# Third pair's right-half weight sums on VectorE, GpSimd's accumulates in program order, and every output transfer on SyncE's queue

## The chip, the cores and the metric

The kernel runs on one NeuronCore of one Trainium2 chip. The metric is the device time of one launch in microseconds (us), as a median over timed runs; lower is better. A core has five engines with queues of their own: PE (TensorE, matrix products), DVE (VectorE), ACT (ScalarE), POOL (GpSimd) and SP (SyncE, here only a queue that issues transfers). Each works through its own instructions in order and waits on semaphores that others raise. Sixteen DMA engines carry the transfers that SP, ACT and POOL issue.

## What is computed

A decoder layer for one sequence of 512 tokens and width 1024. Only its end matters here, the feed-forward part:

```
h = rmsnorm(x, g_pre_ffn) * (1.0 + sc2) + sh2
u = relu(h @ w_ff1)                    # 512 x 4096
y = (u * u) @ w_ff2                    # 512 x 1024, in float32
x = x + ga2 * rmsnorm(y, g_post_ffn)   # the output
```

## The kernel before, in words

All matrix products keep float32 accuracy by splitting each operand into a rounded high part and a rest: `split` (L111 to L113) lets ACT write the high part (L112) and DVE the rest (L113), and PE multiplies high by high, high by rest and rest by high.

The last product, with `w_ff2`, is done by a seven-product (Strassen-like) scheme over 2 x 2 blocks. The 4096 inner rows are 16 **pairs** p = 0 to 15 (`NP`). Its first stage makes four products of each pair (24 matmuls of 128x512), its second stage the other three (18 matmuls). Before the matmuls of a pair, `first_ops(p)` (L869) prepares the operands:

- `ah`: the token side, split from the tile `ub` (whose blocks A11, S1, S3, S2 were written by earlier steps);
- `h1, l1`: split of the left half of the weights `x = xw[p]`, and of the sum `t2` (L882, written over blocks A11 and S1 of `ub`);
- `h2, l2`: split of `n = nw[p]`, the sum of the pair's weights and of its right-half weights (`w_right[p]`). It feeds the second and third product of the pair (p5 and p7); the first (p1) needs only `ah` and the left half of `h1, l1`.

The sum `n` is made in two ways. For pairs 0 and 1 both terms are loaded by SP into `st` tiles (`stage`, L106, three buffers in rotation) and DVE adds them (L878). For pairs 2 to 15, `column_sums(p)` (L864) lets ACT copy the loaded weights into a `wn` tile (L866, three buffers) and POOL issue a transfer that adds `w_right[p]` into it in flight (L867): an accumulating transfer of 512 KB. `load(j)` loads the weights of step j, 512 KB, through SP.

`fourth_sum(p)` (L898) is another accumulating transfer of POOL, of 256 KB, into blocks A11 and S1 of the pair's `ub`, once the first stage of that pair has read them; `second_ops(p)` (L901) needs it in the second stage.

In this part of the kernel the order of DVE, ACT and PE is the order of the code (`manual_schedule`, L840). POOL is not in that list: the framework places its instructions where they can go by its own reckoning, so that a `fourth_sum` stands behind the weight sums of about the same time, though the code calls it much later. SP's transfers stand in the order of the code.

At the end, `end` (L1007) scales and adds one of the four token tiles in two halves on DVE (L1011) and sends each half off at once (L1012): the first half through SP's queue, the second through ACT's. ACT's other work there is the sum of squares of the next halves (`square`, L960), one line of which DVE's next step waits for.

Of the kernel before, what the change touches and what calls it, by code (L numbers as in the profile page):

```python
# [37 lines left out]
WBUF = 4  # L38
LAST = 3
NP = MF // 2  # L40
HB = L // 2
A11, S1, S3, S2, A12, A22 = range(6)
EARLY = 4
# [21 lines left out]
def layer_kernel(tc, x, ada, vecs, c_row, rope, w_first, w_v, w_b, w_a, w_gate, w_up, w_out, w_ff1, w_ff2, w_right, out):  # L65
    nc = tc.nc
    es = ExitStack()
    with es:
# [5 lines left out]
        def uid(name):  # L74
            cnt[0] += 1
            return f"{name}_{cnt[0]}"
# [29 lines left out]
        def stage(src, w=D):  # L106
            st = per.tile([P, D], F32, name=uid("st"), tag="st", bufs=3)
            nc.sync.dma_start(st[:, :w], src)
            return st
# [112 lines left out]
        m_es = ExitStack()  # L222
# [408 lines left out]
        m_es = ExitStack()  # L631
# [22 lines left out]
        for m in range(KT):  # L654
# [5 lines left out]
            for ps, oh, ol, c0 in ((pb, obh, obl, 512), (pa, oah, oal, 0)):  # L660
                for k in range(4):
                    cs = slice(c0 + k * P, c0 + (k + 1) * P)
# [35 lines left out]
        x1 = [x1p.tile([P, D], F32, name=f"x1_{t}") for t in range(NT)]  # L698
# [91 lines left out]
        def block_tile(name, dt):  # L790
            return u2p.tile([P, 6 * HB], dt, name=uid(name), tag="ub", bufs=NP)

        blocks = [block_tile("ub", F32) for p in range(NP)]
        f2p = es.enter_context(tc.tile_pool(name="f2p", bufs=1, side="right"))
# [3 lines left out]
        def blk(p, a, n=1):  # L798
            return blocks[p][:, a * HB:(a + n) * HB]

# [36 lines left out]

        f3p = es.enter_context(tc.tile_pool(name="f3p", bufs=1))
        m_es = ExitStack()
        m_es.enter_context(tc.manual_schedule(engines={mybir.EngineType.DVE, mybir.EngineType.Activation, mybir.EngineType.PE}))  # L840
        p1, p6, p5, p7 = [[bank(a), bank(b)] for a, b in (("tr", "tr"), ("s", "o"), ("s", "s"), ("mm", "mm"))]
        H0, H1 = slice(0, 512), slice(512, D)

# [15 lines left out]
        xw, nw, firsts, seconds = {}, {}, {}, {}  # L859

        def load(j):
            xw[j] = stage(w_ff2[2 * j]) if j < NP else stage(w_ff2[2 * (j - NP) + 1])

        def column_sums(p):  # L864
            nw[p] = ntile().bitcast(F32)
            nc.scalar.activation(nw[p], xw[p], AF.Copy)  # L866
            nc.gpsimd.dma_start(nw[p], w_right[p], accum_op=ALU.add)  # L867

        def first_ops(p):  # L869
            a = pair_tile(p, "ah")  # L870
            x, n = xw[p], nw[p]
            (h1, l1), (h2, l2) = wtile(), wtile()
            t2 = blk(p, 0, 2)
            if p != 1:
                split(a[:, 0], a[:, 1], blk(p, 0, 4))
            split(h1[:, H0], l1[:, H0], x[:, H0])
            if p < 2:
                nc.vector.tensor_tensor(n, n, x, op=ALU.add)  # L878
            if p == 1:
                split(h2, l2, n)  # L880
                split(a[:, 0], a[:, 1], blk(p, 0, 4))
            nc.vector.tensor_tensor(t2, n[:, H1], x[:, H0], op=ALU.add)  # L882
            if p != 1:
                split(h2, l2, n)
            split(h1[:, H1], l1[:, H1], t2)
            nc.vector.tensor_tensor(blk(p, S2), blk(p, A12), blk(p, S2), op=ALU.add)  # L886
            firsts[p] = (a[:, 0], a[:, 1]), (h1, l1), (h2, l2)

        def first_products(p):
            a, w1, w2 = firsts.pop(p)  # L890
            order = [(p1, A11, w1, H0), (p5, S1, w2, H0), (p7, S3, w2, H1), (p6, S2, w1, H1)]
            if p in (0, NP - 1):
                order = [order[i] for i in ((0, 1, 3, 2) if p == 0 else (0, 3, 1, 2))]
            for acc, b, w, cs in order:
                for i in range(2):
                    product(acc, i, a, b * HB, w, cs, p == 0, p == NP - 1)

# [3 lines left out]
        def second_ops(p):  # L901
            if p:
                a = block_tile("a2", F32R)
                ah, al = a[:, :3 * HB], a[:, 3 * HB:]
            else:
                a = pair_tile(0, "ah")
                ah, al = a[:, 0, :3 * HB], a[:, 1, :3 * HB]
            y, n, w = xw[NP + p], ntile(), wtile()
            t2 = blk(p, 0, 2)
# [5 lines left out]
        def second_product(acc, c0, w, cs, p, i):  # L915
            a = seconds[p][0]
            product(acc, i, a, c0 * HB, seconds[p][w], cs, False, p == NP - 1, True)

# [7 lines left out]
        nw[1] = stage(w_right[1])  # L926
        load(2)
        for p in range(NP):
            if p + 1 < NP:
                first_ops(p + 1)  # L930
                if p == 0:
                    load(3)
                    column_sums(2)
            if p == NP - 1:
                second_ops(0)
            load(p + 4)
            if 0 < p < NP - 3:
                if p == 1:
                    column_sums(3)
                column_sums(p + 3)  # L940
            for i in range(2 * (p - NP + 3), 2 * (p - NP + 4)):
                if i >= 0:
                    fourth_sum(i)
            first_products(p)
# [39 lines left out]
        ov = out.rearrange("(t p) d -> t p d", p=P)  # L984
# [22 lines left out]
        def end(t, last, bias):  # L1007
            r = rstd_of(last, bias)
            for n in range(2):
                cs = (H0, H1)[n]  # L1010
                nc.vector.scalar_tensor_tensor(x1[t][:, cs], parts[t, n], r, x1[t][:, cs], op0=ALU.mult, op1=ALU.add)  # L1011
                (nc.sync, nc.scalar)[n].dma_start(ov[t][:, cs], x1[t][:, cs])  # L1012

        def end_low(t):
            parts[t, 1] = c22[:, t % 2]
# [96 lines left out]
```

## Time and profile before

| | us |
|---|---|
| median of 3 timed runs (806.66 to 810.06) | 808.34 |
| the profiled execution | 806.59 |
| its span in the trace | 804.8 |
| PE busy | 767.5 (95%) |
| DVE busy | 593.3 (74%) |
| ACT busy | 416.7 (52%) |
| POOL busy | 29.3 (4%) |

The span is cut by PE's matmuls: the first stage of the seven-product scheme runs from 631.3 to 728.8 us, the second to 794.4, and what is left to 804.8 is DVE's and ACT's end of the norm with the output transfers. PE is the bound wherever its matmuls follow each other without a gap; a gap in them names the place where something else bounds. In a row of the trace, the first two numbers are start and duration in us, and the square bracket at its end is how long the engine had been idle and what ended it.

### The profile page before, as it was taken

The numbers are of one execution on the slowest core, as the hardware profiler recorded it, in microseconds if no ns is written. First come the engines' busy times: TensorE is split into PE (matmuls) and PEld (weight loads), VectorE is DVE, ScalarE is ACT, GpSimd is POOL, SyncE is SP. The second block draws the span as 40 slices with busy tenths as digits, with TensorE's granted clock in tenths as the row PEclk, the third lists the DMA queues.
The fourth block names the chain that finished last, engine by engine and source line by source line (L and its number), as shares of the span: only waits on it lengthen the run. The fifth ranks groups of instructions, "written<-read, shape, count | busy, mean of one in ns | idle before, by whom it ended". The sixth has DMA issues, their size and how long they took to land.

```text
span 804.8 us, 10879 instructions
## 1 busy us (share of the span) xinstructions
PE 767.5 (95%) x4014; PEld 636.4 (79%) x4014; DVE 593.3 (74%) x1111; ACT 416.7 (52%) x753; POOL 29.3 (4%) x45
## 2 busy tenths in 40 slices
PE   6999999989899999999999999999999979999994
PEld 5889977668889887887678998888888758778883
DVE  6876799999957677787866965555545567889866
ACT  6555657564637668622336843322322366768742
POOL 0000000000000000000000000000000122320000
PEclk9999999999999999999999999999999999999998
DMA  9943201122131210477782343444332489996312
GB/s 353 382 120 105 79 27 53 54 78 80 54 105 53 79 53 27 137 258 251 256 301 79 105 131 109 153 157 142 120 104 73 94 172 232 229 235 190 136 54 104
DMA packets 32596, 111.17 MB, mean 138 GB/s; under 512 B 3872, under 2 KB 3872, under 8 KB 32544
## 3 DMA queue, kind: packets, MB, share of 16 engines
q1 hardware_dynamic: 27504, 97.87, 35.4%
q0 software_dynamic: 4320, 11.54, 8.2%
q10 hardware_dynamic: 720, 1.08, 0.4%
q8 instruction: 31, 0.51, 0.3%
q14 instruction: 21, 0.17, 0.1%
HBM read 108.38 MB, written 2.10 MB: 137 GB/s over the span
## 4 chain that ended last, share of the span: by engine, by line
PE 59%; DVE 17%; DMA 10%; issue 8%; ACT 3%; POOL 2%; SPq 0%; ACTq 0%; DVEq 0%; POOLq 0%
PE mm L139 23%; PE s L139 18%; PE o L139 6%; PE mm L857 3%; DVE wlo L113 3%; DVE a L485 3%; DMA wn<-in_w_right_dram 3%; PE s L857 2%; DVE isc L411 2%; DVE sm L410 2%; DMA st<-in_ada_dram 2%; PE tr L857 2%; DMA st<-in_w_gate_dram 2%; ACT whi L112 2%; DVE be L487 2%
## 5 line engine op out<-in xcount | busy, mean ns | idle before, releaser
L112 ACT ACTIVATE whi<-st 128x1024 fp32r<-128x1024 f32 (+3 forms) x118 | 116.3, 988 | 162.1 <-DMA st<-in_w_up_dram 43.2
L113 DVE TENSOR_TENSOR wlo<-st,whi 128x1024 fp32r<-128x1024 f32 (+3 forms) x118 | 133.6, 1135 | 63.1 <-ACT whi L112 62.9
L139 PE MATMUL mm<-hTh,whi 128*128 128x512 f32 x192 | 78.2, 407 | 0.1
L139 PE MATMUL mm<-hTh,wlo 128*128 128x512 f32 x192 | 75.3, 392 | 0.0
L139 PE MATMUL mm<-hTl,whi 128*128 128x512 f32 x192 | 75.1, 391 | 0.0
L139 PE MATMUL mm<-whi,hTh 128*128 128x256 f32 (+2 forms) x208 | 62.2, 305 | 0.1
L212 DVE CUSTOM_DVE_ANT_0 st<-st,cb,vec 128x1024 f32<-128x1024 f32 x32 | 40.8, 1283 | 27.5 <-DMA st<-in_ada_dram 27.4
L139 PE MATMUL mm<-whi,hTl 128*128 128x256 f32 (+2 forms) x208 | 60.2, 295 | 0.0
L139 PE MATMUL mm<-wlo,hTh 128*128 128x256 f32 (+2 forms) x208 | 60.1, 295 | 0.0
L139 PE MATMUL s<-h2h,whi 128*128 128x512 f32 (+1 forms) x120 | 43.4, 361 | 0.0
L139 PE MATMUL s<-h2l,whi 128*128 128x512 f32 (+1 forms) x120 | 43.3, 361 | 0.0
L139 PE MATMUL s<-h2h,wlo 128*128 128x512 f32 (+1 forms) x120 | 43.3, 361 | 0.0
L139 PEld LDWEIGHTS mm<-hTh,wlo 128*128 128x128 f32 x192 | 36.0, 188 | 7.7
L139 PEld LDWEIGHTS mm<-hTh,whi 128*128 128x128 f32 x192 | 36.2, 189 | 6.6 <-DVE qT L523 0.3
L857 PE MATMUL s<-whi,ah 128*128 128x512 f32 x100 | 37.0, 400 | 4.3 <-ACT whi L112 4.3
L139 PEld LDWEIGHTS mm<-hTl,whi 128*128 128x128 f32 x192 | 36.2, 188 | 6.2
L139 PEld LDWEIGHTS mm<-wlo,hTh 128*128 128x128 f32 x208 | 39.5, 190 | 1.0
L139 PEld LDWEIGHTS mm<-whi,hTl 128*128 128x128 f32 x208 | 39.5, 190 | 0.6
L139 PEld LDWEIGHTS mm<-whi,hTh 128*128 128x128 f32 x208 | 39.0, 190 | 0.7 <-ACT ka L546 0.3
L899 POOL DMA_DIRECT2D ub<-in_w_ff_dram x16 | 18.4, 1152 | 539.7 <-DVE ub L886 518.5
L139 PE MATMUL s<-kT,qT 128*128 128x256 f32 (+2 forms) x128 | 30.9, 346 | 2.1 <-ACT be L484 1.8
L113 DVE TENSOR_TENSOR ah<-ub,ah 128x1024 fp32r<-128x1024 f32 (+1 forms) x17 | 20.5, 1209 | 13.4 <-ACT ah L112 13.4
(352 smaller groups left out, 1947.1 us busy)
## 6 DMA issues: line engine op xcount, KB each, us to landing
st<-in_w_ff_dram SPq DMA_DIRECT2D x64, 512.0 KB, 3.6
st<-in_ada_dram SPq DMA_DIRECT2D x32, 512.0 KB, 4.1
sa<-in_ada_dram SPq DMA_DIRECT2D x16, 512.0 KB, 8.3
st<-in_w_gate_dram SPq DMA_DIRECT2D x16, 512.0 KB, 3.4
wn<-in_w_right_dram POOLq DMA_DIRECT2D x14, 512.0 KB, 7.2
st<-in_w_first_dram SPq DMA_DIRECT2D x8, 512.0 KB, 8.7
st<-in_w_b_dram SPq DMA_DIRECT2D x8, 512.0 KB, 3.3
st<-in_w_a_dram SPq DMA_DIRECT2D x8, 512.0 KB, 3.2
```

The source lines that it names most:

```text
L112: nc.scalar.activation(dst_hi, src, AF.Copy)
L113: nc.vector.tensor_tensor(dst_lo, src, dst_hi.bitcast(F32), op=ALU.subtract)
L139: nc.tensor.matmul(o, lhsT, rhs, start=start, stop=stop)
L212: nc.vector.tensor_tensor_reduce(out=st, in0=st, in1=cb[0], scale=1.0, scalar=vec[:, j:j + 1], op0=ALU.mult, op1=ALU.add, accum_out=mod[:, ...
L410: nc.vector.max(out=m8, in_=cur)
L411: nc.vector.match_replace(out=cur, in_to_replace=m8, in_values=cur, imm_value=SENT)
L485: nc.vector.tensor_tensor_scan(a[:, n - 1::-1], a[:, n - 1::-1], zero.to_broadcast([P, n]), 1.0, op0=ALU.mult, op1=ALU.add)
L487: nc.vector.tensor_tensor(be[:, :n - 1], be[:, :n - 1], a[:, 1:n], op=ALU.mult)
L857: nc.tensor.matmul(acc[i], s[:, ts], m[:, cs], start=f, stop=l, skip_group_check=onto)
L899: nc.gpsimd.dma_start(blk(p, 0, 2), w_ff2[2 * p + 1][:, H0], accum_op=ALU.add)
```

## The change

Three edits go together.

1. Pair 2 joins pairs 0 and 1: its `w_right[2]` is loaded by SP into an `st` tile and DVE adds (L878 runs three times, not twice). ACT's copy and POOL's accumulate for that pair are gone. The loads around it are reordered: `w_right[2]` now stands between the loads of pair 2 and pair 3, so that pair 3's and pair 4's weights arrive one place later in the rotation of `st`. ACT's copy for pair 3 now stands ahead of `first_ops(2)`, and the one for pair 4 ahead of `first_ops(3)`.
2. POOL joins the engines in code order.
3. All eight output transfers go through SP.

```
+BY_DVE = 3
-        m_es.enter_context(tc.manual_schedule(engines={mybir.EngineType.DVE, mybir.EngineType.Activation, mybir.EngineType.PE}))
+        m_es.enter_context(tc.manual_schedule(engines={mybir.EngineType.Pool, mybir.EngineType.DVE, mybir.EngineType.Activation, mybir.EngineType.PE}))
...
-            if p < 2:
+            if p < BY_DVE:
                 nc.vector.tensor_tensor(n, n, x, op=ALU.add)
...
         for p in range(NP):
+            if p in (1, 2):
+                column_sums(p + 2)
             if p + 1 < NP:
                 first_ops(p + 1)
-                if p == 0:
-                    load(3)
-                    column_sums(2)
+            if p == 0:
+                nw[2] = stage(w_right[2])
+                load(3)
+            elif p == 1:
+                load(4)
+                load(5)
             if p == NP - 1:
                 second_ops(0)
-            load(p + 4)
-            if 0 < p < NP - 3:
-                if p == 1:
-                    column_sums(3)
-                column_sums(p + 3)
+            if p > 1:
+                load(p + 4)
+                if p + 3 < NP:
+                    column_sums(p + 3)
...
-                (nc.sync, nc.scalar)[n].dma_start(ov[t][:, cs], x1[t][:, cs])
+                nc.sync.dma_start(ov[t][:, cs], x1[t][:, cs])
```

POOL's queue before, at the start of the first stage (`wn` from `w_right` is a weight sum, `ub` from `w_ff` a fourth sum; the numbers in names count tiles, `ub_4761` being pair 0's):

```order
L899 DMA ub_4761<-in_w_ff_dram 128x512
L899 DMA ub_4762<-in_w_ff_dram 128x512
L867 DMA wn_6093<-in_w_right_dram 128x1024
L867 DMA wn_6139<-in_w_right_dram 128x1024
L867 DMA wn_6142<-in_w_right_dram 128x1024
L899 DMA ub_4763<-in_w_ff_dram 128x512
L867 DMA wn_6186<-in_w_right_dram 128x1024
L899 DMA ub_4764<-in_w_ff_dram 128x512
```

From there the two kinds alternate to the end. After the change the queue holds 13 weight sums in a row and then 16 fourth sums; at the place where they meet it reads:

```order
L868 DMA wn_6538<-in_w_right_dram 128x1024
L868 DMA wn_6582<-in_w_right_dram 128x1024
L868 DMA wn_6626<-in_w_right_dram 128x1024
L900 DMA ub_4761<-in_w_ff_dram 128x512
L900 DMA ub_4762<-in_w_ff_dram 128x512
L900 DMA ub_4763<-in_w_ff_dram 128x512
```

So every fourth sum moved behind the last weight sum (pair 15's).

ACT's queue before, from the end of `first_ops(1)` through `first_ops(2)` to the two copies behind it (`whi` from `st`, `wn` or `ub` is a high part):

```order
L112 ACTIVATE whi_6076<-ub_4762 128x512
L866 ACTIVATE wn_6093<-st_6073 128x1024
L112 ACTIVATE ah_6122<-ub_4763 128x1024
L112 ACTIVATE whi_6123<-st_6073 128x512
L112 ACTIVATE whi_6125<-wn_6093 128x1024
L112 ACTIVATE whi_6123<-ub_4763 128x512
L866 ACTIVATE wn_6139<-st_6091 128x1024
L866 ACTIVATE wn_6142<-st_6096 128x1024
```

The same place after the change:

```order
L113 ACTIVATE whi_6076<-ub_4762 128x512
L867 ACTIVATE wn_6119<-st_6093 128x1024
L113 ACTIVATE ah_6122<-ub_4763 128x1024
L113 ACTIVATE whi_6123<-st_6073 128x512
L113 ACTIVATE whi_6125<-st_6091 128x1024
L113 ACTIVATE whi_6123<-ub_4763 128x512
L867 ACTIVATE wn_6166<-st_6138 128x1024
L113 ACTIVATE ah_6169<-ub_4764 128x1024
```

The copy at the same place now reads pair 3's weights (`st_6093`), not pair 2's, and pair 2's high part comes from an `st` tile. SP's queue there, after the change (`st_6091` is `w_right[2]`, `st_6093` pair 3's weights, `st_6138` and `st_6140` those of pairs 4 and 5):

```order
L109 DMA st_6073<-in_w_ff_dram 128x1024
L109 DMA st_6091<-in_w_right_dram 128x1024
L109 DMA st_6093<-in_w_ff_dram 128x1024
L109 DMA st_6138<-in_w_ff_dram 128x1024
L109 DMA st_6140<-in_w_ff_dram 128x1024
```

Before, the place of `st_6091` here was held by pair 3's weights and that of `st_6093` by pair 4's.

ACT's last instructions before:

```order
L175 ACTIVATE sm_7267<-sm_7242,stat 128x1
L1012 DMA out_dram<-x_3_4284 128x512
L961 ACTIVATE jk_6798,sm_7284<-tr_6041 128x512
L961 ACTIVATE jk_6798,sm_7297<-yg_7274 128x512
L175 ACTIVATE sm_7301<-sm_7284,sm_7263 128x1
L1012 DMA out_dram<-x_0_4281 128x512
L961 ACTIVATE jk_6798,sm_7317<-tr_6042 128x512
L175 ACTIVATE sm_7320<-sm_7317,sm_7297 128x1
L1012 DMA out_dram<-x_1_4282 128x512
```

After the change the `out_dram` rows are gone from ACT and stand in SP's queue, which holds nothing but output transfers there.

## Rows read from the trace of the kernel before

**Rows 1.** Busy time by stretch: bounds, length, engines, granted clock, DMA share, GB/s

```profile
642.32:661.45 19.13, 13.34 (x49) 9.85 (x48) 10.38 (x14) 10.27 (x13) 4.41 (x5) 0.91 0.81 172
661.45:728.77 67.32, 66.98 (x289) 53.36 (x288) 55.17 (x74) 49.47 (x63) 19.31 (x22) 1.00 1.01 228
728.77:794.40 65.63, 65.62 (x289) 53.79 (x287) 51.88 (x66) 41.28 (x63) 0.00 (x0) 1.00 0.34 119
794.40:804.80 10.40, 0.00 (x0) 0.00 (x0) 5.55 (x11) 1.89 (x6) 0.00 (x0) 0.70 0.26 102
```

**Rows 2.** Chain that ended last, one piece of the second stage: start, us, work

```profile
743.90 1.36 PE mm L857 x6
```

**Rows 3.** Timeline of PE in pairs 2 and 3, to pair 4's first matmul

```profile
647.66 0.50 PE L857 MATMUL s<-whi,ah 128*128 128x512 f32 x1 [3.82 <-ACT whi L112]
648.92 0.79 PE L857 MATMUL s<-wlo,ah 128*128 128x512 f32 x1 [0.76 <-DVE wlo L113]
...
657.47 0.50 PE L857 MATMUL s<-wlo,ah 128*128 128x512 f32 x1 [0.76 <-DVE wlo L113]
...
661.45 0.39 PE L857 MATMUL tr<-whi,ah 128*128 128x512 f32 x1
```

**Rows 4.** Timeline of ACT: copies of L866, and pair 2's high part

```profile
636.49 1.04 ACT L866 ACTIVATE wn<-st 128x1024 f32<-128x1024 f32 x1
...
646.55 1.06 ACT L112 ACTIVATE whi<-wn 128x1024 fp32r<-128x1024 f32 x1 [7.56 <-DMA wn<-in_w_right_dram]
...
656.58 1.04 ACT L866 ACTIVATE wn<-st 128x1024 f32<-128x1024 f32 x1
...
661.61 1.04 ACT L866 ACTIVATE wn<-st 128x1024 f32<-128x1024 f32 x1
```

**Rows 5.** Timeline of DVE in pair 4: the sum t2 and the rest of n

```profile
660.35 0.68 DVE L882 TENSOR_TENSOR ub<-wn,st 128x512 f32<-128x512 f32 x1
660.95 1.22 DVE L113 TENSOR_TENSOR wlo<-wn,whi 128x1024 fp32r<-128x1024 f32 x1
```

**Rows 6.** DVE's addition for pairs 0 and 1 (ns, min/median/max)

```profile
L878 DVE TENSOR_TENSOR st<-st,st x2: 1219/1220/1220, 615.4 to 626.3; 128x1024 f32<-128x1024 f32 x2
```

**Rows 7.** SP's two issues at 635.98, and landings of st loads, 600 to 660

```profile
635.98 1.35 SPq L108 DMA_DIRECT2D st<-in_w_ff_dram  x2
DMA to landing us min/median/max: 3.1/3.5/6.1
```

**Rows 8.** Landings of L867's accumulates, 645 to 660 us

```profile
DMA to landing us min/median/max: 5.4/5.5/7.2
```

**Rows 9.** DMA view, 661.45 to 719.5 us: queues (packets, MB, share), one issue row

```profile
q0 software_dynamic: 2931, 8.05, 78.8%
q1 hardware_dynamic: 1440, 5.24, 23.1%
...
st<-in_w_ff_dram SPq DMA_DIRECT2D x10, 512.0 KB, 6.8
```

**Rows 10.** Timeline of DVE at the end: scaling and output sums

```profile
792.12 0.74 DVE L1011 SCALAR_TENSOR_TENSOR x<-c,sm,x 128x512 f32<-128x512 f32 x1
794.06 0.69 DVE L1000 TENSOR_TENSOR yg<-tr,ga2b 128x512 f32<-128x512 f32 x1 [1.19 <-ACT jk L961]
...
796.58 1.42 DVE L1011 SCALAR_TENSOR_TENSOR x<-yg,sm,x 128x512 f32<-128x512 f32 x2
799.19 0.69 DVE L1000 TENSOR_TENSOR yg<-tr,ga2b 128x512 f32<-128x512 f32 x1 [1.19 <-ACT jk L961]
...
799.99 1.42 DVE L1011 SCALAR_TENSOR_TENSOR x<-yg,sm,x 128x512 f32<-128x512 f32 x2
```

**Rows 11.** Timeline of ACT at the end: squares and the last issue

```profile
793.34 0.60 ACT L961 ACTIVATE jk<-tr 128x512 bf16<-128x512 f32 x1 [2.12 <-DVE x L1011]
...
798.47 0.60 ACT L961 ACTIVATE jk<-tr 128x512 bf16<-128x512 f32 x1 [2.12 <-DVE x L1011]
...
801.43 0.34 ACTq L1012 DMA_DIRECT2D out_dram<-x  x1
```

## The prediction, as it was made

> **What bounds the kernel now.** I read the busy times by stretch first [rows 1]. From 642 us to the last matmul at 794.4 us PE is the engine to follow, so I ask what each stretch costs beyond its matmuls. Six matmuls that follow each other without a gap take 1.36 us [rows 2], so one takes 0.2267 us, a pair of the first stage (24) 5.44 us and one of the second (18) 4.08 us. Pairs 2 and 3 should take 10.88 us and take 19.13: 8.25 lost. Pairs 4 to 15 (12 x 5.44 = 65.28) take 67.32: 2.04 lost. The second stage (16 x 4.08 = 65.29) takes 65.63, and its last matmul alone outlasts its start by more than the difference: nothing lost. Behind PE's end stand 10.40 us in which DVE works 5.55 and ACT 1.89.
>
> The timeline of PE shows the 8.25 [rows 3]: 3.82 us until ACT has written pair 2's high part, then 0.76 until DVE has the rest, and the same in small for pair 3. The timeline of ACT says why [rows 4]: it copied pair 2's weights at 636.49, and the next high part could only be made at 646.55, after 7.56 us in which it waited for POOL's accumulate. The 2.04 in pairs 4 to 15 belongs to the DMA engines: their share there is 1.01 [rows 1]. Accumulates take 78.8% of 58.04 us for 8.05 MB, 5.68 us per MB, plain loads 23.1% for 5.24 MB, 2.56 per MB [rows 9]. A pair moves a load (0.524 MB, 1.34 us), a weight sum (2.98) and a fourth sum (0.262 MB, 1.49): 5.81 us, more than PE's 5.44.
>
> **Part 1: pair 2's sum by DVE.** It removes an ACT copy and one 512 KB accumulate and adds one DVE addition, 1.22 us [rows 6]. But the chain gets a new start. ACT's copy for pair 3 stands ahead of all of `first_ops(2)`, and it reads a load that SP issues right behind `w_right[2]`, at about 636.3: the two places at 635.98 exist already, filled with other loads [rows 7]. Queued behind that copy on ACT are pair 2's `ah` and both high parts, and DVE waits for these. A load lands in 3.5 us at the median [rows 7]; with one of 1.34 us ahead of it and its issue 0.4 later I take 4.5, so L3 = 640.8. The bounds are 3.1, the shortest, and 6.1, the longest [rows 7]. I stay near the median because the accumulates beside it (pair 1's fourth sum, pair 2's weight sum) are gone from that moment.
>
> From the copy to the end of the rest of n, a pair that waits for nothing takes, in the trace, 660.95 + 1.22 - 656.58 = 5.59 us [rows 4, 5]. Pair 2 has DVE's addition in front of that, 1.14 (its spacing on a busy DVE), and ACT's high part can't run beside t2 any more but follows the addition, some 0.5: 7.3. So pair 2's n is whole at 648.1, against 648.9 before [rows 3]: only 0.8 us are won there, since a load has taken the place of the accumulate as what is waited for. 17 matmuls are left from that point: pair 2 ends at 652.0.
>
> Pair 3 has the same gate a second time. Pair 4's load needs the `st` tile that t2 of pair 2 frees: 660.35 + 0.68 - 656.58 = 4.45 after a copy [rows 4, 5], plus the addition, so it is issued at 646.4 and lands, at 3.5, at 649.9. ACT copies it, then does `first_ops(3)`: n's rest ends 5.6 later, at 655.5. Pair 3's accumulate, issued at 642.4, lands in 5.4 to 7.2 us [rows 8] and is in time. Before, pair 4 began 661.45 - 657.47 = 3.98 us after the matmul that took n's rest [rows 3]; so now at 659.5, **1.9 us** earlier. With both loads at 6.1 it would be 663.7, 2.2 us later than before; with both at 3.1, some 3 us earlier. Whether PE's clock falls (granted 0.91 over the stretch before [rows 1]) moves pair 2's end, but not pair 3's, which hangs on its own load.
>
> **Part 2: POOL in code order.** In pairs 4 to 15 the fourth sums leave the DMA engines: 1.34 + 2.98 = 4.32 us a pair, under PE's 5.44. The next limit is the round of ACT and DVE, 661.61 - 656.58 = 5.03 us where nothing blocks it [rows 4], also under 5.44. So PE's gaps should close: **2.0 us**, bounds 0.3 and 2.04. The price is that 16 fourth sums (16 x 1.49 = 23.8 us of all DMA engines) follow the last weight sum. PE is at pair 12 then, near 706, and that sum lands by 715. With a quarter of the engines' time going to loads, a fourth sum then takes 2.0 us and number k lands at 717 + 2k; the second stage wants it at 724.8 + 4.08k, less some 3 us of preparation. The slack is 5 us and grows.
>
> **Part 3: outputs through SP.** An issue costs its queue 0.34 us [rows 11], and that is not the point. ACT's issue waits for the half that DVE is still scaling, and the square behind it waits along: ACT idles 2.12 us twice, and after each DVE idles 1.19 for the square [rows 10, 11]. Without the issues ACT can square at 793.34 - 2.12 = 791.2, before DVE's L1011 ends at 792.86, so DVE goes on at once: 1.2 us, and again 1.2 at 799.19, where the square then ends near 796 and DVE arrives at 796.8. Sum **2.4 us**; bounds 1.2, if one of the two idles is taken over by another wait, and 2.5. SP has nothing else to issue there, and its issues come 0.7 us or more apart.
>
> The Trainium skill speaks against this part: its page "DMA: Bandwidth & Descriptors", section "Issuing engines are not separate DMA queues", says that issuing from several engines saves only the issue time. By that, the move would be worth two issues on ACT, 0.7 us, and the whole sum would be 4.6. The rows show a wait in front of the issue that the rule doesn't speak of.
>
> **The sum** is 1.9 + 2.0 + 2.4 = 6.3 us. The profiled execution took 806.59 (span 804.8 and 1.8 around it), which is 1.75 under the median of the timed runs and close to the lowest of them; it would become 800.3. Against the median, 808.34 - 6.3 = 802.0.
>
> **Rivals.**
> - *The loads gate ACT.* Both loads that the copies wait for land like the longest, 6.1, not like the median. Pair 4 then starts 2.2 us later than before, and the net is -2.2 + 2.0 + 2.4 = 2.2: 806.1. For it: the two copies have ACT idle until the landing, and the second load can only start when a tile is free. Against it: the 6.1 belongs to a stretch with accumulates beside the loads.
> - *The tail gives only the issue time*: 1.9 + 2.0 + 0.7 = 4.6, 803.7. It needs the idles of 1.19 to stay, and I see nothing that would hold them.
> - *The burst binds.* If the fourth sums and the loads of the second stage slow each other to twice the time, number k lands at 717 + 4k and loads at 6.8 [rows 9] become late; PE would lose some 2 to 4 us at the stage's start: 804 to 806. The skill's same page, section "Queues, rings and completion order", has each DMA engine go round its queues packet by packet. By that a load passes beside a long row of accumulates, at most at half speed; the 6.8 against 3.5 [rows 7, 9] agrees.
> - *Slower.* The same gate as in the first rival, at a worse price: ACT stands in front of the landing twice, and each us of delay in each counts fully. Measured from the 3.5 of the sum, a delay of d each costs 2d; it eats the 6.3 at d = 3.2 and is slower by over 0.5% (4.0 us) from d = 5.2, a landing of 8.7 us. With accumulates of three pairs ahead of the loads that could be; 813. The loaded stretch has a median of 6.8 [rows 9].
>
> **How the numbers follow.** Forecast 0.58; loads gate 0.22; tail small 0.07; burst 0.07; slower 0.06. The likeliest is 802.0. Its own bounds are about 799 to 804; the gate and the burst reach 806.1, and the spread of the timed runs adds some: 799 to 807. A measurement of this kernel can tell about 0.5%, 4.0 us, from no change: under 804.3 counts as faster. That holds for nearly all of the forecast and for the small tail: 0.66. The gate, the burst and the forecast's end are within: 0.28. Slower: 0.06.
>
> **What would show it.** In the changed profile: pair 2's first use of n near 648.1 and pair 4's first matmul near 659.5; ACT idle before two copies of L867 (the new number of that line), put down to an `st` load; no gap of PE from pair 4 on, with a DMA share near 0.8 there and a full one around 710 to 740; no DVE idle put down to the square at the end, and the span behind the last matmul near 8.0, not 10.4. I am wrong if these loads take over 6 us, if the gaps in pairs 4 to 15 stay without fourth sums beside them, or if the second stage shows waits for `ub`.

## The result and the profile after

The changed kernel took 802.0 us (median of five runs, 801.03 to 803.91) against 807.99 us for the kernel before in the same session: a ratio of 0.9927, with a 95% interval of 0.9905 to 0.9949, or 6.0 us. Run a second time, beside other kernels, it took 802.44 against 806.49, 0.9945 [0.9926, 0.9963]. The forecast was 802.0 in a range of 799 to 807, with faster by over 0.5% as the likeliest outcome. The time and the sign came out. The working did not come out in every term, and one part of the change showed no gain that can be told.

The profiled execution took 802.46 us, its span 800.5. The first view is the busy times by stretch, cut at the same events as [rows 1]: from the end of pair 1's matmuls, from pair 4's first matmul, from the second stage's first, and from PE's end. Columns: the stretch and its length, then busy us and instructions of PE, PEld, DVE, ACT and POOL, granted clock, DMA share, GB/s.

```profile
642.95:660.90 17.95, 13.95 (x49) 9.61 (x49) 12.90 (x17) 10.88 (x15) 2.74 (x3) 0.90 0.70 157
660.90:726.18 65.28, 65.28 (x289) 54.05 (x288) 55.26 (x74) 49.44 (x63) 19.25 (x22) 1.00 0.93 208
726.18:791.79 65.61, 65.61 (x289) 53.79 (x287) 52.73 (x67) 41.52 (x64) 3.46 (x4) 1.00 0.55 159
791.79:800.50 8.71, 0.00 (x0) 0.00 (x0) 4.21 (x9) 1.54 (x6) 0.00 (x0) 0.74 0.32 122
```

Beside [rows 1], pairs 2 and 3 take 17.95 instead of 19.13 (1.18 won), pairs 4 to 15 take 65.28 instead of 67.32 (2.04 won, and 65.28 is exactly 12 x 5.44), the second stage 65.61 instead of 65.63, and 8.71 us lie behind PE's end instead of 10.40 (1.69 won). Together that is 4.93 us. The span fell by only 4.3, because the stage itself began 0.6 later (631.95 against 631.32), in a part of the program that the change does not touch. The timed difference of 6.0 has an interval of about 4.1 to 7.7 us, which holds the 4.93.

The head, on PE's timeline (start, duration, engine, line, operation, out<-in, and in brackets the idle time before it and what ended it). It answers to [rows 3]:

```profile
644.72 0.50 PE L858 MATMUL tr<-whi,ah 128*128 128x512 f32 x1 [1.60 <-ACT whi L113]
646.06 0.79 PE L858 MATMUL tr<-wlo,ah 128*128 128x512 f32 x1 [0.84 <-DVE wlo L114]
649.54 0.51 PE L858 MATMUL s<-wlo,ah 128*128 128x512 f32 x1 [0.46 <-DVE wlo L114]
...
653.84 0.50 PE L858 MATMUL tr<-whi,ah 128*128 128x512 f32 x1 [0.17 <-ACT whi L113]
655.18 0.50 PE L858 MATMUL tr<-wlo,ah 128*128 128x512 f32 x1 [0.84 <-DVE wlo L114]
...
660.90 0.39 PE L858 MATMUL tr<-whi,ah 128*128 128x512 f32 x1
```

The idle of 3.82 for pair 2's high part is gone. In its place pair 2 itself starts late (644.72 rather than 642.95) and stalls three times for less. ACT's timeline, beside [rows 4], says why:

```profile
642.14 1.06 ACT L867 ACTIVATE wn<-st 128x1024 f32<-128x1024 f32 x1 [4.93 <-DMA st<-in_w_ff_dram]
643.10 1.04 ACT L113 ACTIVATE ah<-ub 128x1024 fp32r<-128x1024 f32 x1
...
647.17 1.06 ACT L113 ACTIVATE whi<-st 128x1024 fp32r<-128x1024 f32 x1 [2.51 <-DVE st L879]
...
651.26 1.06 ACT L867 ACTIVATE wn<-st 128x1024 f32<-128x1024 f32 x1 [2.51 <-DMA st<-in_w_ff_dram]
```

ACT waits for a plain load before the copies of pairs 3 and 4, where before it waited 7.56 us for the accumulate [rows 4]. The `ah` of pair 2 stands behind the first of these copies, as the prediction said it would.

The waits are not the whole loss of the head. In pairs 2 and 3 PE's idles add up to 5.8 us before (3.82, 0.76, 0.45 and 0.76) and to 3.9 after (1.60, 0.84, 0.46, 0.17 and 0.84). The losses are 8.25 and 7.07 (17.95 - 10.88). What is left, 2.5 and 3.2 us, is matmuls that follow each other more slowly. Most of them stand in a stretch behind the first wait in which the granted clock is 0.50, the lower of TensorE's two levels (1.2 of 2.4 GHz). That stretch in the kernel before, and then after, with the columns of the first view:

```profile
648.40:651.80 3.40, 2.88 (x7) 2.30 (x8) 2.20 (x4) 3.09 (x4) 2.19 (x3) 0.50 0.65 170
```

```profile
645.90:649.20 3.30, 3.02 (x6) 1.78 (x6) 2.87 (x4) 1.58 (x2) 0.00 (x0) 0.50 0.80 148
```

Seven matmuls keep PE busy for 2.88 us there and six for 3.02, where 0.2267 each would be 1.59 and 1.36.

The DMA engines in pairs 4 to 12 and then during the row of fourth sums, two windows of the DMA view (queue: packets, MB, share of 16 engines; issues: count, KB each, median us to landing). They answer to [rows 8, 9]:

```profile
q0 software_dynamic: 1382, 5.01, 62.4%
q1 hardware_dynamic: 1341, 4.90, 26.9%
...
st<-in_w_ff_dram SPq DMA_DIRECT2D x10, 512.0 KB, 3.5
wn<-in_w_right_dram POOLq DMA_DIRECT2D x9, 512.0 KB, 5.5
```

```profile
ub<-in_w_ff_dram POOLq DMA_DIRECT2D x16, 256.0 KB, 14.5
st<-in_w_ff_dram SPq DMA_DIRECT2D x6, 512.0 KB, 7.9
```

Without fourth sums beside them, loads land in 3.5 us instead of 6.8 [rows 9]. Once the 16 fourth sums stand in a row they land in 14.5 and the loads in 7.9. ACT waits 4.5 us in all for those loads, at four places, and PE does not stand still once in the stretch.

The tail, first on DVE's timeline, then on ACT's, beside [rows 10, 11]:

```profile
790.18 0.68 DVE L1005 TENSOR_TENSOR yg<-tr,ga2b 128x512 f32<-128x512 f32 x1
...
794.02 0.68 DVE L1005 TENSOR_TENSOR yg<-tr,ga2b 128x512 f32<-128x512 f32 x1
...
794.81 1.42 DVE L1016 SCALAR_TENSOR_TENSOR x<-yg,sm,x 128x512 f32<-128x512 f32 x2
```

```profile
788.52 0.57 ACT L966 ACTIVATE jk<-tr 128x512 bf16<-128x512 f32 x1
...
792.37 0.58 ACT L966 ACTIVATE jk<-tr 128x512 bf16<-128x512 f32 x1
```

Both idles of 1.19 in front of DVE's `yg<-tr` are gone, because ACT now makes each square before DVE comes to it. DVE's last operation ends 4.44 us behind PE's end (796.23 less 791.79) instead of 7.00. But what follows DVE's end grew from 3.36 to 4.22, and the view of the output line shows where: the landing times of the eight output transfers, of the kernel after.

```profile
DMA to landing us min/median/max: 2.0/2.0/3.2
```

Before, it read 2.0/2.0/2.1. One transfer, the last, now takes 1.1 us longer, which gives back 0.86 of the 2.56.

### The profile page after: what moved, and what is told of

Read it like the earlier page. It is cut to its first block, busy times and chain, and to the rows that moved or that the text cites. A ratio compares the mean times of both kernels' runs of the same rounds, so it can differ in the third digit from the quotient of the medians.

```text
span 800.5 us, 10875 instructions
## 1 busy us (share of the span) xinstructions
PE 767.6 (96%) x4014; PEld 638.4 (80%) x4014; DVE 593.9 (74%) x1112; ACT 415.0 (52%) x752; POOL 28.3 (4%) x44
## 4 chain that ended last, share of the span: by engine, by line
PE 71%; DVE 17%; DMA 7%; issue 2%; ACT 2%; SPq 0%; DVEq 0%; ACTq 0%
PE mm L140 25%; PE s L140 19%; PE o L140 6%; PE s L858 6%; PE mm L858 5%; PE tr L858 4%; DMA st<-in_ada_dram 3%; DVE wlo L114 3%; DVE a L486 3%; DVE isc L412 2%; DVE sm L411 2%; DMA st<-in_w_gate_dram 2%; PE tr L430 2%; DVE be L488 1%; PE tr L140 1%
## 5 line engine op out<-in xcount | busy, mean ns | idle before, releaser
L868 POOL DMA_DIRECT2D wn<-in_w_right_dram x13 | 11.4, 876 | 594.3 <-ACT wn L867 551.2
```

## The experiments

The words used below: edit 1 is the weight sum of pair 2 by DVE with the loops written out anew, edit 2 is GpSimd in code order, edit 3 the outputs through SP. All lengths in this table are read from the timelines of PE and DVE, in us. The first column is the time from the stage's first matmul to pair 4's first. The second is pairs 4 to 15. The third is DVE's end behind PE's end, and the fourth is what lies from there to the last instruction. The second stage took 65.60 to 65.66 in all of them.

| kernel | to pair 4 | pairs 4 to 15 | DVE's end | rest | ratio [95% interval] |
|---|---|---|---|---|---|
| before | 30.13 | 67.32 | 7.00 | 3.36 | 1 |
| after | 28.95 | 65.28 | 4.44 | 4.22 | 0.9927 [0.9905, 0.9949] |
| after_again | 29.00 | 65.28 | 4.44 | 4.13 | 0.9945 [0.9926, 0.9963] |
| p1_sum_by_dve | 30.46 | 65.28 | 7.00 | 3.12 | 1.000 [0.9982, 1.0017] |
| p2_pool_order | 28.61 | 65.28 | 7.00 | 4.22 | 0.9974 [0.9963, 0.9985] |
| p3_outputs_sp | 30.47 | 68.32 | 4.44 | 3.34 | 0.9975 [0.9961, 0.9989] |
| skip_odd_fourth | 29.25 | 65.28 | 7.00 | 3.15 | one run |
| no_dve_sum | 29.01 | 65.28 | 4.44 | 4.19 | 0.9936 [0.9910, 0.9961] |
| copy_behind | 29.12 | 65.28 | 4.44 | 4.13 | 0.9932 [0.9907, 0.9957] |
| four_by_dve | 22.70 | 71.47 | 4.44 | 4.17 | 0.9951 [0.9933, 0.9969] |
| last_by_act | 29.01 | 65.28 | 4.44 | 4.14 | 0.9936 [0.9923, 0.9949] |
| pad_dve | 29.77 | 65.28 | 4.44 | 3.08 | 0.9930 [0.9916, 0.9944] |
| four_pad | 22.67 | 72.03 | 4.43 | 2.99 | 0.9938 [0.9920, 0.9956] |
| no_sum_pad | 29.26 | 65.28 | 4.44 | 3.12 | 0.9930 [0.9906, 0.9954] |

The kernel before took 807.99 us beside the row after, and 806.49 to 807.49 beside the others. The head is not the same to the last tenth from execution to execution: after, after_again and pad_dve have the same instructions there and show 28.95 to 29.77. One reason is the clock: it is granted at 0.50 from 645.9 to 649.2 us in after, and from 649.1 to 655.8 in pad_dve, where pair 3 follows pair 2 without a gap. Differences of less than about 0.8 in the first column therefore decide nothing.

### Each edit alone

**Edit 1 alone**, on the kernel before:

```
-            if p < 2:
+            if p < BY_DVE:
...
         for p in range(NP):
+            if p in (1, 2):
+                column_sums(p + 2)
...
+            if p == 0:
+                nw[2] = stage(w_right[2])
+                load(3)
```

> The first edit alone: pair 2's sum by DVE with the loads in their new order; the fourth sums stay between the weight sums, the outputs stay on two queues. Theory (two loads gate ACT): PE still loses 7 to 8 us in pairs 2 and 3, with ACT idle before the first two copies put down to an st load, and the 2.0 us of pairs 4 to 15 stay, since a pair's transfers still add up to 5.81 us; the time is 0 to 1.5 us under before. Rival (the accumulate was what cost the time and all of its 7.56 us go): 4 to 6 us under before.

Measured: 806.98 against 807.49, no difference that can be told. ACT's wait for the load and PE's gaps in that run:

```profile
643.66 1.06 ACT L867 ACTIVATE wn<-st 128x1024 f32<-128x1024 f32 x1 [6.29 <-DMA st<-in_w_ff_dram]
...
652.74 1.06 ACT L867 ACTIVATE wn<-st 128x1024 f32<-128x1024 f32 x1 [2.46 <-DMA st<-in_w_ff_dram]
```

```profile
646.24 0.79 PE L858 MATMUL tr<-whi,ah 128*128 128x512 f32 x1 [2.96 <-ACT whi L113]
647.58 0.79 PE L858 MATMUL tr<-wlo,ah 128*128 128x512 f32 x1 [0.55 <-DVE wlo L114]
651.07 0.79 PE L858 MATMUL s<-wlo,ah 128*128 128x512 f32 x1 [0.47 <-DVE wlo L114]
```

With a fourth sum still beside the load, ACT waits 6.29 for it, not 4.93, and pair 4 starts no earlier than before. The first load landed 6.5 us after its issue and the second 3.3, so the rival "the loads gate ACT" holds here for the first load only. PE's idles are just 3.98 of the 8.58 us that pairs 2 and 3 lose. Most of the rest is the clock, granted at 0.50 over this stretch:

```profile
646.24:655.50 9.26, 8.24 (x18) 5.52 (x18) 6.01 (x8) 4.34 (x6) 1.73 (x2) 0.50 0.81 183
```

Eighteen matmuls keep PE busy for 8.24 us there, where 18 x 0.2267 would be 4.08. Pair 3 then starts without a gap, so pair 4's start hangs on PE at that clock. The second load gates little less. Counted from ACT's second copy as in the changed kernel (660.90 - 651.26 = 9.64), an estimate, pair 4 could have started at 662.38, and it started at 662.57. The steady stretch surprised me: it took 65.28, although the fourth sums were still interleaved with the pairs. Its busy times by stretch, from pair 4's first matmul on:

```profile
662.57:680.00 17.43, 17.43 (x78) 14.45 (x77) 15.26 (x21) 14.16 (x18) 5.49 (x7) 1.00 1.05 243
680.00:700.00 20.00, 20.00 (x90) 16.54 (x89) 16.47 (x22) 14.94 (x19) 6.81 (x8) 1.00 1.04 247
700.00:727.85 27.85, 27.85 (x124) 23.06 (x123) 23.45 (x32) 20.87 (x28) 7.01 (x8) 1.00 0.97 233
```

The kernel before, from 680 to 700 us:

```profile
680.00:700.00 20.00, 19.83 (x85) 15.39 (x85) 15.48 (x21) 15.38 (x19) 7.03 (x8) 1.00 1.06 246
```

The DMA engines are as full as before (1.04 against 1.06 from 680 to 700 us), and PE stands nowhere: 90 matmuls in these 20 us against 85. So a full DMA share by itself did not make PE wait. What fits is lead: by the prediction's figures each pair with a fourth sum falls behind by 5.81 - 5.44 = 0.37 us, some 4 us in eleven pairs, and edit 1 puts a load of 1.34 us of the DMA engines in the place of an accumulate of 2.98. PE's slow matmuls in the kernel before begin only at 683, some 22 us into the stretch. But ACT's waits for accumulates in p1_sum_by_dve do not grow steadily: 0.78 at 661 and 0.46 at 671, then 0.67, 0.63 and 1.19 from 708 to 720. The lead itself was not varied, so this reading is argued and not shown.

**Edit 2 alone:**

```
-        m_es.enter_context(tc.manual_schedule(engines={mybir.EngineType.DVE, ...
+        m_es.enter_context(tc.manual_schedule(engines={mybir.EngineType.Pool, mybir.EngineType.DVE, ...
```

> The second edit alone: only the fourth sums move behind the weight sums. Theory (the DMA engines' volume set the pace of pairs 4 to 15): the loss of 2.04 us there falls to under 0.3, and pair 2's accumulate lands about 1 us earlier since pair 1's fourth sum is not ahead of it; 2 to 3.5 us under before, and no wait for a fourth sum in the second stage. Rival (the burst behind the weight sums takes it back): no change within 1 us, with PE waiting in the second stage.

Measured: 804.95, 2.5 us less than before. It wins the 2.04 of the steady stretch, and it also wins 1.5 us in the head, where I had given it nothing. GpSimd's timeline in the kernel before, and then with edit 2 alone:

```profile
637.62 0.87 POOL L899 DMA_DIRECT2D ub<-in_w_ff_dram  x1 [13.37 <-DVE wlo L113]
638.15 1.22 POOL L867 DMA_DIRECT2D wn<-in_w_right_dram  x1
```

```profile
638.98 1.01 POOL L867 DMA_DIRECT2D wn<-in_w_right_dram  x1 [533.74 <-DVE ub L886]
```

And ACT's wait for that accumulate, and PE's for ACT, with edit 2 alone:

```profile
646.18 1.06 ACT L112 ACTIVATE whi<-wn 128x1024 fp32r<-128x1024 f32 x1 [6.05 <-DMA wn<-in_w_right_dram]
```

```profile
647.29 0.50 PE L857 MATMUL s<-whi,ah 128*128 128x512 f32 x1 [2.31 <-ACT whi L112]
```

Before, a fourth sum was issued right ahead of pair 2's accumulate and shared the DMA engines with it. The accumulate's landing, the longest of its line in the head, falls from 8.4 to 7.4 us, and ACT waits 6.05 instead of 7.56 [rows 4]. The same head starts pair 4 at 29.01 in no_dve_sum and 29.26 in no_sum_pad, so the gain is 0.9 to 1.5 us. skip_odd_fourth below, in which that fourth sum (pair 1's) is left out, shows 29.25. This covers the head's gain of the whole change (1.18), and it comes from an edit that I had costed for the steady stretch only.

**Edit 3 alone:**

```
-                (nc.sync, nc.scalar)[n].dma_start(ov[t][:, cs], x1[t][:, cs])
+                nc.sync.dma_start(ov[t][:, cs], x1[t][:, cs])
```

> The third edit alone: all outputs through SP. Theory (ACT's issue waits for DVE's half and holds the square behind it): DVE's two idles of 1.19 us go, DVE ends 2.4 to 2.8 us earlier behind PE's last matmul, and the last transfer decides what is left of it: 1.5 to 2.8 us under before. Rival (only the issue time is saved): 0.7 us.

Measured: 805.3, 2.2 us less. DVE's end moves from 7.00 to 4.44 behind PE's end, and here nothing is given back: the rest stays at 3.34 and all outputs land in 2.0 to 2.1 us. The steady stretch of this one profile was longer than before (68.32), in a part that the edit does not touch.

### Is it the volume of the fourth sums?

On the kernel before, without the fourth sums of the odd pairs, which its result then lacks:

```
         def fourth_sum(p):
-            nc.gpsimd.dma_start(blk(p, 0, 2), w_ff2[2 * p + 1][:, H0], accum_op=ALU.add)
+            if p % 2 == 0:
+                nc.gpsimd.dma_start(blk(p, 0, 2), w_ff2[2 * p + 1][:, H0], accum_op=ALU.add)
```

> The kernel before, with the fourth sums of the odd pairs left out (their part of the result is missing): half the volume of the fourth sums goes, and they still stand between the weight sums. Theory (volume on the DMA engines): a pair moves 5.07 us of transfers on average, under PE's 5.44, and the loss of 2.04 us in pairs 4 to 15 goes to under 0.5. Rival (each weight sum is held up by the fourth sum issued ahead of it in POOL's order): about half of the loss stays.

Measured: pairs 4 to 15 in 65.28, the 2.04 gone, one time of 805.46. So the loss ends when half of the fourth sums' bytes are taken out of the DMA engines. In p1_sum_by_dve, where all of them stay in the stretch, it ends too, so it hung by a small margin. For that reason the run does not rule out that the place of a fourth sum ahead of a weight sum in GpSimd's order has a share in it.

### Does DVE's sum add anything to the other two?

**The change without edit 1** (edits 2 and 3 on the kernel before), and the change run again beside it:

> The second and third edit without the first. Of the single edits, the first gave nothing by itself. Theory (the first edit trades a wait for an accumulate against two waits for loads): the first stage is as long as in the changed kernel, within 1 us, or up to 1 us shorter, and the time is within 1 us of the changed kernel's. Rival (the first edit pays only once the fourth sums are out of the way): 1.5 to 2 us slower than the changed kernel.

> The changed kernel once more, beside the others of this call, for comparison on the same chip: 802 us, 0.992 to 0.994 of the kernel before; the last output lands in 2.0 to 3.2 us.

Measured: 801.41 without DVE's sum and 802.44 with it, intervals that overlap widely. Pair 4 starts at 29.01 and at 29.00. PE's gaps without DVE's sum:

```profile
644.86 0.49 PE L857 MATMUL s<-whi,ah 128*128 128x512 f32 x1 [2.72 <-ACT whi L112]
646.12 0.50 PE L857 MATMUL s<-wlo,ah 128*128 128x512 f32 x1 [0.76 <-DVE wlo L113]
653.40 0.50 PE L857 MATMUL s<-whi,ah 128*128 128x512 f32 x1 [0.15 <-ACT whi L112]
654.66 0.50 PE L857 MATMUL s<-wlo,ah 128*128 128x512 f32 x1 [0.76 <-DVE wlo L113]
```

One gap of 2.72 for the accumulate stands where the changed kernel has 1.60, 0.84 and 0.46. The end is the same: no worth of edit 1 beside edit 2 can be told. Edits 2 and 3 alone took 2.5 and 2.2 us off, 4.7 together, and the kernel with both took 5.1 off (806.49 - 801.41).

### Where does the head's loss go?

If pair 2 is late in the changed kernel only because the copy for pair 3 stands ahead of its work on ACT, then moving the copy behind that work should free pair 2. The question is whether the gain stays. On the kernel after:

```
-            if p in (1, 2):
-                column_sums(p + 2)
+            if p == 2:
+                column_sums(4)
             if p + 1 < NP:
                 first_ops(p + 1)
+            if p == 1:
+                column_sums(3)
```

> The changed kernel, with ACT's copy of pair 3's weights put behind first_ops(2), not ahead of it; the copy of pair 4 stays ahead of first_ops(3). Theory (what gates pair 2 is the copy in front of it in ACT's order, which waits for a load of another pair): ACT goes on with pair 2 at once, DVE's addition starts when w_right[2] has landed, near 641 on the changed kernel's clock, PE takes pair 2's n near 644.5 instead of 649.5, pair 3 then waits about 3 us for its accumulate, issued near 645, and pair 4 starts 3 to 4 us earlier: 3 to 4 us faster than the changed kernel. Rival (pair 3's accumulate, issued later now, gives it all back): within 1 us of the changed kernel.

Measured: pair 2 starts on time and takes 5.81, but pair 3 takes 12.31, and pair 4 starts at 29.12. ACT and PE in pair 3:

```profile
652.65 1.06 ACT L113 ACTIVATE whi<-wn 128x1024 fp32r<-128x1024 f32 x1 [3.79 <-DMA wn<-in_w_right_dram]
```

```profile
653.76 0.79 PE L858 MATMUL s<-whi,ah 128*128 128x512 f32 x1 [2.08 <-ACT whi L113]
```

The accumulate, issued behind the later copy, is now what is waited for. Of the 6.87 us that pair 3 loses, PE's idles are 3.4; most of the rest falls into a stretch from 653.0 to 659.7 us with a granted clock of 0.50. The gain went to the next pair, whole.

**Pair 3's sum by DVE too**, so that the first accumulate is pair 4's. On the kernel after, `BY_DVE = 4`, with loads and copies moved accordingly:

```
-BY_DVE = 3
+BY_DVE = 4
...
+            if p < 2:
+                nw[p + 2] = stage(w_right[p + 2])
+                load(p + 3)
+            elif p == 2:
                 load(5)
+                column_sums(4)
+                load(6)
+                column_sums(5)
```

> The changed kernel, with pair 3's sum by DVE as well (its w_right loaded by SP) and no copy of ACT ahead of first_ops(2) and first_ops(3). So the first accumulate is pair 4's. Theory (whichever pair is first to need an accumulate pays for the way from load over copy to landing, about 10 us, less what PE has queued): pairs 2 and 3 run with under 1 us lost, pair 4 loses 3 to 4 us, and pair 5 starts 3 to 4 us earlier than in the changed kernel; 3 to 4 us faster. Rival (the first accumulate costs the same 7 us wherever it stands): equal to the changed kernel within 1 us.

Measured: 802.95, no better than the change. Pair 4 starts at 22.70, 6.25 earlier, and pairs 4 to 15 take 71.47, 6.19 longer. PE's gaps and ACT's wait:

```profile
649.47 0.50 PE L858 MATMUL s<-wlo,ah 128*128 128x512 f32 x1 [0.27 <-DVE wlo L114]
...
655.04 0.50 PE L858 MATMUL tr<-wlo,ah 128*128 128x512 f32 x1 [0.84 <-DVE wlo L114]
...
658.46 0.51 PE L858 MATMUL s<-whi,ah 128*128 128x512 f32 x1 [1.97 <-ACT whi L113]
659.72 0.65 PE L858 MATMUL s<-wlo,ah 128*128 128x512 f32 x1 [0.75 <-DVE wlo L114]
```

```profile
657.35 1.06 ACT L113 ACTIVATE whi<-wn 128x1024 fp32r<-128x1024 f32 x1 [3.71 <-DMA wn<-in_w_right_dram]
```

The first accumulated pair is late again, by as much. Adding the first two columns of the table gives the whole first stage. It is 94.23 with the change, 94.29 without DVE's sum, 94.40 with the copy behind, 94.17 with two sums by DVE: four arrangements of the head within 0.23 us of each other. That they agree so closely is in part chance, since the same arrangements in other profiles give 93.89 (p2_pool_order) and 95.05 (pad_dve). All four are some 7.2 over the 16 x 5.44 = 87.04 of bare matmuls. Of these 7.2, PE's idles are 3.4 to 4.4, and the rest is mostly matmuls at a granted clock of 0.50 behind a wait, which none of the four was without. What sets the waits stays open: the three `st` buffers, through which every load of this stage goes, and the accumulates' own landing are left as candidates, and I tried neither. Nor did I try whether shorter waits would leave the clock up.

### What holds the last output?

**The last output by ACT's queue**, on the kernel after:

```
-                nc.sync.dma_start(ov[t][:, cs], x1[t][:, cs])
+                (nc.scalar if (t, n) == (1, 1) else nc.sync).dma_start(ov[t][:, cs], x1[t][:, cs])
```

> The changed kernel, with the very last half sent off by ACT's queue, behind which ACT has no work. In the profile of the changed kernel the last transfer took 3.2 us from issue to landing, the others 2.0. If two halves 0.66 us apart in one queue cost that, it lands in 2.0 here and the kernel is 0.8 to 1.2 us faster than the changed one; if the 3.2 was a chance of that one execution, the two are equal within 0.4 us. DVE's two idles must stay away either way, since no square stands behind this issue.

Measured: 801.51, rest 4.14, and the last output still lands in 3.1. SP's queue is not the cause. Edit 2 alone also has the late landing (rest 4.22), with its outputs on two queues as before, and edit 3 alone has not. The DMA view of the last 4.5 us shows what the late ones have in common. The changed kernel:

```profile
q1 hardware_dynamic: 288, 0.52, 30.5%
q14 instruction: 1, 0.01, 0.4%
...
out_dram<-x SPq DMA_DIRECT2D x1, 256.0 KB, 3.2
```

One transfer of instructions, a single packet of 8 KB, runs beside the last output. Before, p1_sum_by_dve, p3_outputs_sp and skip_odd_fourth have none in these microseconds. If such a fetch belongs to DVE's instruction stream, then more instructions of DVE at the start of the program must shift it to another place. So I added eight one-column memsets of DVE to three kernels. They run from 3.24 us on, in an idle of DVE: its next operation starts at 4.36 in pad_dve and at 4.42 in the changed kernel. The three are the changed kernel, four_by_dve, and no_dve_sum.

```
         nc.gpsimd.memset(eps, EPS)
+        for _ in range(8):
+            nc.vector.memset(eps, EPS)
```

> The changed kernel, with eight one-column memsets on DVE at its start (they rewrite a constant with its own value). In the six profiles so far in which the last output took 3.1 to 3.2 us to land, an 8 KB code transfer ran 2.4 to 2.5 us before the span's end; each of these kernels has one more instruction in DVE's record (1346) than the four without it (1334 to 1345), whose last output took 2.0. Theory (DVE's code crosses a block right at its end, and that fetch holds up the last output): the fetch comes some us earlier, the last output lands in 2.0 and the span behind DVE's last instruction is 3.1 to 3.4 us, not 4.2; 0.5 to 1 us faster than the changed kernel, less up to 0.5 us for the memsets. Rival (the fetch belongs to something else): 4.1 to 4.3 us behind DVE's last instruction as before.

> Pair 3's sum by DVE as well and the eight memsets at DVE's start, together. If the two theories hold, 4 to 5 us faster than the changed kernel, 797 to 798 us; if neither does, 802.

> The kernel before with edits 2 and 3 (GpSimd in code order, all outputs through SP), without DVE's sum of pair 2, and with eight one-column memsets of DVE added at the program's start. Without the eight, the length from the stage's first matmul to the end of the span was 168.6 us against 173.4 before, and 4.19 us lay behind DVE's end. If the 8 KB instruction transfer inside the last output is what makes that output land at 3.2 rather than 2.0, and if DVE's additional instructions move it: 3.0 to 3.2 us behind DVE's end, a length near 167.5, and 800.3 to 801.0 against a kernel before of 806.8. If the landing has another cause: 4.1 to 4.2 us behind DVE's end, and 801.4. That DVE's sum is worth nothing beside edit 2 is expected by both: pair 4 starts 28.6 to 29.8 us after the stage's first matmul, as with it (28.95).

Measured: the rest is 3.08, 2.99 and 3.12 instead of 4.22, 4.17 and 4.19. The DMA view of the last 4.5 us of no_sum_pad has no fetch, and both outputs in it land in 2.0:

```profile
q1 hardware_dynamic: 467, 0.83, 47.6%
...
out_dram<-x SPq DMA_DIRECT2D x2, 256.0 KB, 2.0
```

The fetch has not vanished but moved: an earlier output of the same kernel is now the slow one, where nothing waits for it (landing of its eight outputs):

```profile
DMA to landing us min/median/max: 2.0/2.0/2.9
```

In all fourteen profiles the rest is 4.13 to 4.22 where the fetch falls into the last output and 2.99 to 3.36 where it does not. That the place depends on DVE's instructions is shown; why one packet of 8 KB delays the output by 1.1 us is not. In the timed runs the gain can't be separated: pad_dve took 800.97 against the change's 802.0 and 802.44, four_pad 801.91 against 802.95, but no_sum_pad 801.3 against 801.41, where I had expected 800.3 to 801.0. Intervals of 0.15 to 0.25% don't resolve 1.1 us of 800. None of these versions is measurably better than the change itself; no_dve_sum does as well with less code.

## Why the prediction was right, point by point

**Part 1, 1.9 us: the size was too large and the cause was wrong.** Pair 4 started 1.18 us earlier, which lies within the bounds (-2.2 to +3), and the picture of the gate is what the trace shows: ACT idle before two copies of L867, put down to the loads. But three steps failed. First, the prediction said that PE's timeline shows all of the 8.25 us as waits; its idles there are 5.8, and the other 2.5 are mostly matmuls at a granted clock of 0.50. It also let the clock move pair 2's end only; in p1_sum_by_dve and pad_dve pair 3 starts without a gap and hangs on PE at that clock, not on its own load. Second, the load for pair 3 was in use 5.15 us after its issue (636.99 to 642.14), where I took 4.5; counted from the stage's start, n of pair 2 was whole at 17.59 (649.54 - 631.95) instead of the forecast 16.78 (648.1 - 631.32), and pair 4 started at 28.95 instead of 28.2. Third, I costed this part against the kernel before with its fourth sum ahead of pair 2's accumulate, though Part 2 takes that one away. By itself Part 1 shows no gain in time (1.000), and beside Part 2 none either (29.01 without, 28.95 to 29.00 with). The gain that I had put down to it belongs to Part 2. The prediction's favourable bound was also mis-added: with both loads at 3.1 its own chain has pair 4 start 3.7 us earlier (661.45 less 657.7), not some 3.

**Part 2, 2.0 us: right in size, and short of a term.** The 2.04 came back to the last hundredth, and without half of the bytes it comes back too (skip_odd_fourth). The DMA share fell only to 0.90 up to 710 us, not to 0.8: the accumulates took 6.1 us per MB (62.4% of 48.93 us for 5.01 MB), not the 5.68 that the sum used. What the part left out is the head's 0.9 to 1.5 us. What it overstated is its own necessity: p1_sum_by_dve loses nothing in that stretch either, so the 2.04 must not be counted for both parts.

**The burst** of fourth sums was worse for the loads than the rival's price: 7.9 us to landing where the rival took 6.8, and 14.5 for a fourth sum. PE still lost nothing, because the slack that the prediction counted was there: 65.61 in the second stage. The mechanism was right; that it would bind was not.

**Part 3, 2.4 us: right at DVE, less at the end.** DVE's end moved by 2.56, both idles of 1.19 and a little more. The rival "only the issue time" falls: edit 3 alone took 2.2 us off the time, not 0.7. The Trainium skill's page "DMA: Bandwidth & Descriptors", section "Issuing engines are not separate DMA queues", says that issuing from several engines saves only the issue time. Here the measurement differs from what follows if it is read the other way round: to take the issues from ACT was worth three times the two issues, since each waited in ACT's order for a half that DVE was still scaling. The net tail, 1.69, is short of the forecast by the 0.86 that the last output's landing gave back, through a cause that nothing in the profile of before showed.

**The sum** of 6.3 met a timed 6.0 (and 4.1 in the second session) and 4.93 in the trace. The terms erred by 0.7 each in the head and the tail, in the same direction. That the time met 802.0 to the tenth is therefore luck: the sum was 1.4 too large by the trace, and it was taken from 808.34, where the kernel before later took 806.49 to 807.99. "Loads gate ACT" was partly true: the first load landed in 5.1 us, nearer to 6.1 than to the median of 3.5, and the second in 3.3. In p1_sum_by_dve, where the fourth sums remain beside them, it was 6.5 and 3.3, and pair 4 started 0.3 us later than before, not the rival's 2.2. The slower rival needed landings of 8.7 us, and no load of the head came near.

## What to carry to other kernels

Cost each part of a change against the kernel that has the other parts, not against the kernel before: here two parts removed the same 2.04 us, and the head's gain came from the part that seemed to concern another stretch. A loss at the start of a pipelined stage that moves from pair to pair when it is treated (some 7.2 us in four arrangements) may have a cause that they share, so look for that before rearranging further. Add up the engine's idles first: here they were about half of that loss, and the rest was mostly the clock behind them. A transfer that waits for another engine's result should be issued by an engine that has nothing else in its order.

## What the runs showed of the hardware that I had not expected

- An 8 KB instruction fetch in the last microseconds went with an output landing of 3.1 to 3.2 us instead of 2.0; eight more instructions of DVE at the program's start moved it to an earlier output, which then landed in 2.9. Small edits can thus shift the end by 1.1 us for no reason of their own.
- DMA engines with a share of 1.04 to 1.05 over 37 us cost PE nothing in p1_sum_by_dve, while a share of 1.01 over 67 us went with a loss of 2.04 before.
- Behind a wait of PE at the stage's start, all fourteen profiles show a stretch with a granted clock of 0.50. In p1_sum_by_dve 18 matmuls kept PE busy for 8.24 us there instead of 4.08, and that took more from the head than the waits did (3.98).
- A plain 512 KB load landed in 3.5 us at the median beside weight sums alone, and in 7.9 beside a row of fourth sums.
